# RMSNorm and matmul on one core: a reordered opening, a third load cut in two, and a last tile stored in two blocks

## The chip, the core and the metric

The kernel runs on one core of one Trainium2 chip. The metric is the device time of one execution in microseconds (us), median of several runs. The profile shows one execution; its span is some 1.8 us shorter than the time of the same run. A run's state is "fast" or "slow", or "unknown" where a kernel ran only once; the slow ones are left out of comparisons.

## The reference

```python
batch, seq, dim, out_dim = 16, 1024, 512, 768
rms = np.sqrt(np.mean(x ** 2, axis=-1, keepdims=True) + eps)
x_norm = x / rms * gamma
return np.matmul(x_norm, weight).astype(np.float32)
```

x has 16384 rows of 512 floats. The kernel works on 128 tiles of 128 rows. It reads 35 MB and writes 50 MB.

## The kernel before

Gamma is multiplied into the weights once, and each row's 1/rms is applied to the finished product. So a tile of x needs a cast to bf16, transposes on TensorE (PE), eight matmuls (four chunks of 128 rows of weights, each in a block of 512 and one of 256 columns), and one scaling on its way from PSUM to the output tile. PE can only start on the real work when the first weights have been loaded, cast and multiplied. This is the opening:

```python
    opening = [1, 2, 1, 2, 2]
    x_first, x_size = stretches(XG, {0: opening + [4, 4], 1: [4, 4, 8]})
    o_first, o_size = stretches(OG, {0: opening, 1: [4, 4], last - 1: [4, 4], last: [2, 2, 2, 1, 1]})
    ...
        load_until(3)                      # x tile 0, then tiles 1 and 2 in one load
        for h in range(2):                 # then the two halves of the weights
            nc.sync.dma_start(out=w_f32[:, 2 * h:2 * h + 2, :].rearrange("p c o -> p (c o)"), in_=wv[:, h, :])
        load_until(2 * XG)
    ...
        weights(0, nc.vector, 0, WIDE)     # chunk 0 on DVE, in two blocks
        weights(0, nc.vector, WIDE, O)
        weights(1, nc.scalar)              # chunk 1 on ACT
        for k in (0, 1):
            for i in range(3):
                matmuls(i, acc[i], [k])
        root(0, 3, ssq)
        weights(2, nc.vector)
        weights(3, nc.scalar)
        ...
        matmuls(0, acc[0], [2, 3])
```

x comes in groups of 16 tiles with two buffers, so the third group (tiles 32 to 47) can be loaded only when the first group has been used. All loads of x and weights and all stores go out from SyncE (SP). At the end, tiles 126 and 127 are computed in two column blocks (512 on ACT, 256 on DVE) and stored whole.

## Time and profile before

| what | before |
|---|---|
| time, 6 runs | 210.96 us (210.69 to 211.86) |
| span of the profiled run | 208.6 us |
| PE busy | 199.0 us (95%) |
| first real matmul | 8.67 us |
| end of the last compute | 203.58 us |

The page of the profile cuts the span into 40 slices; a digit is the busy share of one slice in tenths.

### The profile page before, as it was taken

How to read it: one execution, taken by the hardware profiler on the slowest of the kernel's cores; microseconds unless marked ns; L12 is line 12 of the kernel's file. 1: busy time of each engine (PE TensorE's matmuls, PEld its weight loads, DVE VectorE, ACT ScalarE, POOL GpSimd, SP SyncE). 2: the span in 40 equal slices, each digit the busy share in tenths (PEclk: the TensorE clock that was granted, in tenths of full speed). 3: DMA queues.
4: the chain of work that ended last, by engine and by line, in shares of the span. 5: the costliest groups of instructions: out<-in, count | busy, mean ns of one | idle time of the engine just before them, and what ended most of it. 6: DMA issues, size and time to landing. Idle time of an engine off the chain costs nothing.

```text
span 208.6 us, 3553 instructions
## 1 busy us (share of the span) xinstructions
PE 199.0 (95%) x1268; PEld 137.7 (66%) x1293; DVE 111.6 (54%) x204; ACT 158.2 (76%) x388; POOL 65.8 (32%) x71
## 2 busy tenths in 40 slices
PE   7799999999999999999999999999999999999990
PEld 3366777666766776677667666766776667667650
DVE  2555654654564465456546545654664565456450
ACT  4589787787778778777877877787787778778850
POOL 1058532303631343215323063311533054230000
PEclk9999999999999999999999999999999999999999
DMA  6999999999999999999999999999999999899885
GB/s 216 399 431 415 424 398 433 478 408 394 438 448 421 410 438 434 440 412 424 448 437 432 396 438 438 434 412 432 438 427 456 405 424 437 353 443 386 361 349 225
DMA packets 6630, 85.69 MB, mean 411 GB/s; under 512 B 978, under 2 KB 980, under 8 KB 3156
## 3 DMA queue, kind: packets, MB, share of 16 engines
q1 hardware_dynamic: 6336, 85.46, 97.0%
q8 instruction: 10, 0.16, 0.3%
q10 hardware_dynamic: 276, 0.00, 0.1%
q14 instruction: 8, 0.07, 0.1%
HBM read 35.13 MB, written 50.33 MB: 410 GB/s over the span
## 4 chain that ended last, share of the span: by engine, by line
PE 91%; DMA 3%; DVE 1%; ACT 1%; issue 1%; SPq 0%; DVEq 0%
PE ops L156 78%; PE tp L121 13%; DMA w_f<-in_weight_dram 3%; DVE ot L140 1%; ACT ot L138 0%; SPq L83 0%; ACT jk L98 0%; DVE w_bf L140 0%; DVE xT L128 0%; ACT rms L102 0%; DVE rstd L104 0%; DVEq L140 0%
## 5 line engine op out<-in xcount | busy, mean ns | idle before, releaser
L156 PE MATMUL ops<-w_bf,xT 128*128 128x512 bf16 (+1 forms) x999 | 192.5, 324 | 2.8 <-DVE w_bf L140 1.4
L156 PEld LDWEIGHTS <-xT 128*128 128x128 bf16 x1024 | 100.2, 98 | 57.8 <-issue 1.9
L94 POOL CAST xb<-xt 128x1024 bf16<-128x1024 f32 (+1 forms) x65 | 65.1, 1016 | 120.0 <-PE tp L121 62.2
L128 DVE COPY xT<-tp 128x1024 bf16<-128x1024 bf16 (+1 forms) x67 | 44.5, 667 | 81.0 <-PE tp L121 81.0
L138 ACT ACTIVATE ot<-ops,rstd 128x768 f32<-128x768 f32 (+1 forms) x65 | 58.1, 895 | 37.6 <-PE ops L156 36.8
L98 ACT ACTIVATE jk<-xt 128x512 bf16<-128x512 f32 x128 | 78.7, 619 | 1.1 <-DMA xt<-in_x_dram 1.1
L121 PE MATMUL tp<-ident_f,xb 128*128 128x128 f32 x256 | 69.2, 275 | 0.1
L140 DVE TENSOR_SCALAR ot<-ops,rstd 128x768 f32<-128x768 f32 (+1 forms) x65 | 64.5, 992 | 2.9 <-PE ops L156 2.8
L121 PEld LDWEIGHTS tp<-ident_f,xb 128*128 128x128 f32 x256 | 36.1, 142 | 3.8 <-issue 0.7
L98 ACT ACTIVATION_READ_ACCUMULATOR jk<-xt 128x1 f32 x128 | 24.4, 191 | 0.0
L102 ACT ACTIVATE rms<-ssq,eps_sb 128x2 f32<-128x2 f32 (+1 forms) x64 | 18.9, 296 | 2.0
L104 DVE RECIPROCAL rstd<-rms 128x2 f32<-128x2 f32 (+1 forms) x64 | 10.0, 156 | 3.3 <-ACT rms L102 3.2
L211 PE MATMUL ops<-warm 128*128 128x512 bf16 x11 | 4.8, 585 | 1.2 <-DVE eps_sb L204 1.2
L138 ACT ACTIVATE w_bf<-w_f,g_sb 128x768 bf16<-128x768 f32 x2 | 1.9, 936 | 2.6 <-DMA w_f<-in_weight_dram 2.6
L211 PEld LDWEIGHTS <-warm 128*128 128x128 bf16 x11 | 1.4, 134 | 2.6 <-issue 1.4
L193 ACT ACT_TABLE_LOAD x1 | 1.3, 1283 | 1.8 <-issue 1.8
L94 DVE CAST xb<-xt 128x512 bf16<-128x512 f32 x2 | 1.0, 491 | 2.4 <-DMA xt<-in_x_dram 2.4
L140 DVE TENSOR_SCALAR w_bf<-w_f,g_sb 128x512 bf16<-128x512 f32 (+2 forms) x3 | 1.4, 484 | 1.2 <-DMA w_f<-in_weight_dram 1.2
L225 PEld LDWEIGHTS tp<-ident_f,g_row 2*128 2x128 f32 x2 | 0.3, 201 | 0.8 <-issue 0.8
L202 DVE MEMSET warm<- 128x256 uint32 x1 | 0.3, 272 | 0.9 <-PEq L312 0.9
L225 PE MATMUL tp<-ident_f,g_row 2*128 2x2 f32 x2 | 0.4, 264 | 0.0
L227 DVE COPY g_sb<-tp 128x4 f32<-128x4 f32 x1 | 0.2, 161 | 0.4 <-PE tp L225 0.4
(7 smaller groups left out, 1.0 us busy)
## 6 DMA issues: line engine op xcount, KB each, us to landing
out_dram<-ot SPq DMA_DIRECT2D x12, 3072.0 KB, 15.1
xt<-in_x_dram SPq DMA_DIRECT2D x6, 4096.0 KB, 19.2
out_dram<-ot SPq DMA_DIRECT2D x4, 1536.0 KB, 10.8
out_dram<-ot SPq DMA_DIRECT2D x6, 768.0 KB, 9.6
xt<-in_x_dram SPq DMA_DIRECT2D x4, 1024.0 KB, 13.9
xt<-in_x_dram SPq DMA_DIRECT2D x1, 2048.0 KB, 18.8
xt<-in_x_dram SPq DMA_DIRECT2D x3, 512.0 KB, 6.2
w_f<-in_weight_dram SPq DMA_DIRECT2D x2, 768.0 KB, 7.1
```

Source lines behind the costliest of these rows:

```text
L94: engine.tensor_copy(out=xb_tiles[i // 2][:, i % 2:i % 2 + n, :], in_=held(x_tiles, XG, i, n))
L98: nc.scalar.activation(out=jk, in_=held(x_tiles, XG, i)[:, 0, :], func=AF.Square, accum_out=ssq)
L102: nc.scalar.activation(out=rms[:, :n], in_=ssq[:, :n], func=AF.Sqrt, scale=1.0 / D, bias=eps_sb)
L104: nc.vector.reciprocal(out=rstd[:, :n], in_=rms[:, :n])
L121: nc.tensor.transpose(out=tp_tiles[j][:, t, h, :], in_=words[:, lo:lo + P], identity=ident_f)
L128: nc.vector.tensor_copy(out=dst[:, t:t + n, :], in_=src[:, t:t + n, :])
L138: nc.scalar.mul(out=dst, in_=src, mul=r)
L140: nc.vector.tensor_single_scalar(out=dst, in_=src, scalar=r, op=mybir.AluOpType.mult)
L156: nc.tensor.matmul(out=acc[:, lo:hi], lhsT=xT_tiles[i // 2][:, i % 2, k // 2, :, k % 2], rhs=w_bf[:, k, lo:hi], start=(k == 0), stop=(k == ...
L193: nc.scalar.preload_act_table(AF.Sqrt)
L211: nc.tensor.matmul(out=spare[:, :WIDE], lhsT=warm[:, :P], rhs=warm, start=True, stop=True)
L225: nc.tensor.transpose(out=gp[:, c, :], in_=g_row[:, :, c], identity=ident_f[:2, :2])
```

## The change

The intent: the first half of the weights goes ahead of x tile 2, so that PE starts earlier and works on tiles 0 and 1 as they land; the third group of x comes in two loads; and the end is stored in smaller pieces, so that less is left to transfer after the last matmul. Before the weights, a tiny load "touches" them; it now goes ahead of gamma's load. The matmuls that only warm PE up are regrouped too (13 instead of 11; the cut below leaves them out).

```diff
-    opening = [1, 2, 1, 2, 2]
+    opening = [1, 1, 1, 1, 2, 2]
-    x_first, x_size = stretches(XG, {0: opening + [4, 4], 1: [4, 4, 8]})
-    o_first, o_size = stretches(OG, {0: opening, 1: [4, 4], last - 1: [4, 4], last: [2, 2, 2, 1, 1]})
+    x_first, x_size = stretches(XG, {0: opening + [4, 4], 1: [4, 4, 8], 2: [8, 8]})
+    o_first, o_size = stretches(OG, {0: opening, 1: [4, 4], last - 1: [4, 4], last: [2, 2, 1, 1, 1, 1]})
...  (touch of the weights moved ahead of the load of gamma)
+        load_until(2)
+        load_weights(0)
         load_until(3)
-        for h in range(2):
-            nc.sync.dma_start(out=w_f32[:, 2 * h:2 * h + 2, :]...)
+        load_weights(1)
         load_until(2 * XG)
...
         weights(1, nc.scalar)
-        for k in (0, 1):
-            for i in range(3):
-                matmuls(i, acc[i], [k])
+        cast(2, nc.gpsimd)
+        square(2, ssq[:, 2:3])
+        matmuls(0, acc[0], [0, 1])
+        transpose_tile(2)
+        matmuls(1, acc[1], [0, 1])
+        matmuls(2, acc[2], [0, 1])
+        weights(2, nc.vector)
         root(0, 3, ssq)
...
-            store(i)
+                if i == NT - 1:
+                    nc.sync.dma_start(out=rows(out, i, 1)[:, 0, lo:hi], in_=out_tile(i)[:, lo:hi])
+            if i < NT - 1:
+                store(i)
```

More of the change, by code (lines that the diff above doesn't have):

```diff
@@ L186 @@
     with tc.manual_schedule():
-        g_row = singles.tile([2, P, 2], F32)
-        nc.scalar.dma_start(out=g_row, in_=gamma.rearrange("(h w c) -> h w c", w=P, c=2))
         wv = weight.rearrange("(h w c) o -> w h (c o)", w=P, c=2)
@@ L192, with load_weights @@
         nc.scalar.dma_start(out=touched, in_=wv[:, :, 0:1])
+        g_row = singles.tile([2, P, 2], F32)
+        nc.scalar.dma_start(out=g_row, in_=gamma.rearrange("(h w c) -> h w c", w=P, c=2))
         nc.scalar.preload_act_table(AF.Sqrt)
+        w_f32 = singles.tile([P, K, O], F32)
+        def load_weights(h):
+            nc.sync.dma_start(out=w_f32[:, 2 * h:2 * h + 2, :].rearrange("p c o -> p (c o)"), in_=wv[:, h, :])
+        load_until(2)
+        load_weights(0)
         load_until(3)
-        w_f32 = singles.tile([P, K, O], F32)
-        for h in range(2):
-            nc.sync.dma_start(out=w_f32[:, 2 * h:2 * h + 2, :].rearrange("p c o -> p (c o)"), in_=wv[:, h, :])
+        load_weights(1)
         load_until(2 * XG)
@@ L227 @@
         nc.vector.tensor_copy(out=g_sb, in_=gp)
+        cast(1, nc.vector)
+        square(1, ssq[:, 1:2])
         transpose_tile(0)
-        warm_up(3)
-        cast(1, nc.vector)
-        cast(2, nc.gpsimd)
-        square(1, ssq[:, 1:2])
-        square(2, ssq[:, 2:3])
+        warm_up(2)
         transpose_tile(1)
-        transpose_tile(2)
-        warm_up(2)
+        warm_up(5)
         acc = [accumulator() for _ in range(4)]
@@ L241 @@
         weights(1, nc.scalar)
-        for k in (0, 1):
-            for i in range(3):
-                matmuls(i, acc[i], [k])
+        cast(2, nc.gpsimd)
[5 more added lines that the diff above has]
+        weights(2, nc.vector)
         root(0, 3, ssq)
-        weights(2, nc.vector)
         weights(3, nc.scalar)
@@ L250 @@
         finish_tile(0, acc[0], nc.scalar)
+        matmuls(1, acc[1], [2, 3])
         transpose_tile(3)
+        finish_tile(1, acc[1], nc.vector)
         norms(3, 1)
-        matmuls(1, acc[1], [2, 3])
-        finish_tile(1, acc[1], nc.vector)
         cast(4, nc.gpsimd)
```

## The prediction

> **What bounds the kernel now.** I read the page first, for the engine that is full and for the two ends of the row of slices.
>
> ```profile
> PE 199.0 (95%) x1268; PEld 137.7 (66%) x1293; DVE 111.6 (54%) x204; ACT 158.2 (76%) x388; POOL 65.8 (32%) x71
> ...
> PE   7799999999999999999999999999999999999990
> ...
> PE 91%; DMA 3%; DVE 1%; ACT 1%; issue 1%; SPq 0%; DVEq 0%
> ```
>
> TensorE (PE) is busy nine tenths or more of every slice but the first two and the last, and it carries 91% of the chain that ended last. The middle can be checked by windows: 49.63, 49.69 and 39.69 us of PE work in windows of 50, 50 and 40 us. A pair of tiles repeats every 3.03 us whatever the transfers do. So the middle has nothing to give, and I looked only at the time before PE's real work starts and after it stops. The timeline of the first microseconds gives the start:
>
> ```profile
> 6.65 0.59 PE L211 MATMUL ops<-warm 128*128 128x512 bf16 x2
> ...
> 8.12 0.94 ACT L138 ACTIVATE w_bf<-w_f,g_sb 128x768 bf16<-128x768 f32 x1 [1.90 <-DMA w_f<-in_weight_dram]
> 8.13 0.75 DVE L140 TENSOR_SCALAR w_bf<-w_f,g_sb 128x512 bf16<-128x512 f32 x2 [0.75 <-DMA w_f<-in_weight_dram]
> 8.67 1.51 PE L156 MATMUL ops<-w_bf,xT 128*128 128x512 bf16 x8 [1.43 <-DVE w_bf L140]
> ...
> 9.93 0.94 ACT L138 ACTIVATE w_bf<-w_f,g_sb 128x768 bf16<-128x768 f32 x1 [0.68 <-DMA w_f<-in_weight_dram]
> 9.93 0.62 DVE L140 TENSOR_SCALAR w_bf<-w_f,g_sb 128x768 bf16<-128x768 f32 x1 [0.48 <-DMA w_f<-in_weight_dram]
> ```
>
> The columns are start, duration, engine, line, operation, and in brackets the idle time before it with its releaser. PE is idle 1.43 us until the first half of the weights has landed (8.03 to 8.1) and its first block is cast (8.63). From 8.67 on PE does not stop. The second half lands at 9.9 and is cast by 10.55 (DVE, chunk 2) and 10.87 (ACT, chunk 3). PE's six tile halves on the first weights take 6 x 0.325 us (0.216 + 0.108 us for 512 and 256 columns) and end at about 10.62. So PE asks for chunk 2 just 0.07 us after it is ready: **the two arrivals are balanced**, and this decides my estimate.
>
> At the other end I read the timeline and windows of half a microsecond:
>
> ```profile
> 202.67 0.69 ACT L138 ACTIVATE ot<-ops,rstd 128x512 f32<-128x512 f32 x1 [0.61 <-PE ops L156]
> 203.10 0.48 DVE L140 TENSOR_SCALAR ot<-ops,rstd 128x256 f32<-128x256 f32 x1 [0.81 <-PE ops L156]
> ```
> ```profile
> 201.50:202.00 0.50, 0.50 (x5) 0.29 (x3) 0.22 (x2) 0.50 (x1) 0.00 (x0) 1.00 0.72 283
> 202.00:202.50 0.50, 0.50 (x4) 0.23 (x3) 0.29 (x1) 0.06 (x1) 0.00 (x0) 1.00 0.45 184
> 202.50:203.00 0.50, 0.50 (x5) 0.26 (x3) 0.00 (x0) 0.33 (x1) 0.00 (x0) 1.00 1.01 418
> ...
> 206.00:206.50 0.50, 0.00 (x0) 0.00 (x0) 0.00 (x0) 0.00 (x0) 0.00 (x0) 1.00 0.69 264
> 206.50:207.00 0.50, 0.00 (x0) 0.00 (x0) 0.00 (x0) 0.00 (x0) 0.00 (x0) 1.00 0.06 25
> ```
>
> The last two columns are DMA share and GB/s. Compute ends at 203.58, the span at 208.6: 5 us of storing. The transfers run at full rate from 202.5 to 206.3, so there is a backlog, preceded by a hole of some 0.35 us of full work (shares 0.72 and 0.45).
>
> **What the Trainium skill says.** "DMA: Bandwidth & Descriptors", section "Queues, rings and completion order": all copies issued by one sequencer share one ring on each of 16 DMA engines, and each engine consumes its ring in order[...]. It adds that the engines finish independently, so a copy is done when its slowest engine is. The trace agrees with both. In its completion records, 14 of 16 engines had finished the first half of the weights by 6.92 us, the other two at 7.87 and 8.03; for the second half, 14 by 8.79, two at 9.74 and 9.90. The packets show two engines standing still from about 4.8 to 5.9 after one packet of the weights, and carrying that lag of 1.1 us along. The same page, "Anatomy of one DMA", puts a fixed 2 us on a copy, mostly the receipt of the last write (fitted there to the GpSimd path). Here the first x tile, 256 KB, took 2.76 us from issue to use; at the 0.085 us that a 2 KB packet takes, 8 packets per engine are 0.68 us of it, so about 2 us is fixed. "TensorE: Matmul & The Clock Gate", Part 1, says that PE runs at half clock until it has been busy for some 3.4 us; here the warm-up matmuls took 634 ns early and 379 ns late.
>
> **The change part by part.**
>
> *Order of loads.* One tile of x (8 packets of 2 KB per engine, 8 x 0.085 = 0.68 us) goes ahead of the weights in place of two (8 packets of 4 KB, 8 x 0.159 = 1.27). The first half of the weights lands 0.59 us earlier: 8.03 becomes 7.44. Tile 2 then costs 0.68 between the halves, so the second half lands 0.09 later, at about 10.0: nothing was taken out ahead of it.
>
> *Start of PE.* The casts take as long as before (8.03 to 8.67 = 0.64), so the first matmul is at 8.08. Tile 0 runs chunks 0 and 1 at once, and chunk 1 comes from ACT 0.94 + 0.1 us after landing, at 8.48; tile 0 ends its half at 8.81. Tile 2 of x lands at 7.44 + 0.68 = 8.12, its cast on GpSimd takes 0.61, so its transposes fit right after at 8.83 (0.22 us), then tiles 1 and 2 (2 x 0.325 x 2 = 1.3): PE is through at 10.35.
>
> *The wait that replaces it.* Chunk 2 is cast at 10.0 + 0.05 + 0.62 = 10.67, chunk 3 at about 11.0. PE waits some 0.3 us, and finishes tile 0 at about 11.33. Before, it finished tile 0 at 10.62 + 0.65 = 11.27, having done the transposes of tile 2 in the idle time. From there on both kernels have the same PE work. So the opening **gains nothing as long as the second half arrives at 10.0**; the 0.59 us is taken back as 0.3 us of waiting, 0.22 us of transposes moved into the busy stretch and 0.1 us of waiting for chunk 1. Net: +0.05 us.
>
> *Touching the weights first, gamma second.* The touch goes out 0.57 us earlier, as do the weights themselves, so their distance is the same. Gamma used to arrive at 2.8 and PE asked for it at 3.86: about 1 us of slack. Even if it waits behind the 256 tiny pieces of the touch, which landed 3.7 us after issue, it comes near 5, and the second cast is at about 5.3, where it was before (5.25). Cost 0.
>
> *Third group in two loads.* The second half is asked for four pairs later, still six pairs (18 us) before its first cast. PE does not idle there before (23.84 us busy of the 24 after 26 us). Worth 0.
>
> *End.* Tile 124 is stored alone and fills the hole of 0.35 us. The last tile's wide block leaves at 203.4 rather than 203.63, but it queues behind the backlog. Rows of 3, 2 and 1 KB cost a little more per byte (0.121 us for 3 KB against 0.236 for 6 KB, and a further issue of 0.33 us): about 0.1 us back. For most engines this is 0.2 us gained. But the span waits for the last engine: on the final store 15 engines completed by 206.87 and one at 207.65, and that one had no hole (it completed its shares at 203.33, 205.48, 206.75 and 207.65). For it the gain is near 0. I take 0.1.
>
> Sum: +0.05 - 0.1 = -0.05 us, so 210.87 for this reading.
>
> **Rivals.**
>
> *The standstill goes away.* If the two engines stop because the first reads of the weights meet the touch (its 4-byte packets run at 4.0 to 4.6, right before), a changed order could remove it. Then the second half lands at 8.8, chunk 2 is cast at 9.45, PE is through its six halves at about 9.5 (limited by the five warm-ups, until about 7.4), and the gain is 1.1 to 1.3 us: 209.6. For it: the coincidence, and that two engines alone are hit. Against it: touch and weights move together by 0.57 to 0.59 us, and other lags of about 1 us appear later in the run with no touch. I give it 30%.
>
> *Late or cold start.* If gamma arrives after 5.5, or the gap while PE waits for it keeps the clock at half rate, the five warm-ups take 5 x 0.427 = 2.1 us and run into the first real work, or the first matmuls run at half speed: 0.2 to 0.5 us lost, 211.2. For it: fewer warm-ups ahead. Against: PE still has 5 at the end. 10%.
>
> *Lag at the end instead of the hole.* If no engine lags at the end, the last store gains 0.3 us more: 210.5. It adds to either case and widens the lower side.
>
> **Range and chances.** 0.6 x 210.85 + 0.3 x 209.6 + 0.1 x 211.2 = 210.5. The runs of before scatter over 0.3 us. The range covers the second case and the third: 209.4 to 211.2. A gain of 2% would be 4.2 us, almost all of PE's 8.67 us of start; a loss of 2% would need a new stall in the middle. Faster 0.01, same 0.98, slower 0.01.
>
> **What would show it right or wrong.** Right: the first real matmul of PE near 8.1 instead of 8.67; then an idle of about 0.3 us before 10.7, released by the cast of chunk 2; completion of the second half of the weights near 10.0; the same 3.03 us per pair; no hole in the transfers near 202, and compute's end to span's end still 4.8 to 5 us. Wrong: the second half of the weights completing near 8.8 (the standstill gone, gain over 1 us); PE waiting for gamma beyond 5.5; the first matmuls taking twice their time; or any idle of PE in the middle.

## The result

The changed kernel takes 210.82 us (210.66 to 211.39, 6 runs), the kernel before 210.96 us. The ratio is 0.9994, 95% interval 0.9972 to 1.0016: the same. Executions over 1.5% slower than the fastest of the same kernel are left out of the means. A ratio here is the mean time of one kernel's fast runs over that of the other's of the same rounds, so it is not quite the ratio of the medians quoted.

The page of the changed kernel, busy times and chain of waits:

```profile
PE 200.0 (96%) x1295; PEld 137.5 (66%) x1295; DVE 111.5 (53%) x204; ACT 158.3 (76%) x388; POOL 65.8 (31%) x71
...
PE 89%; DMA 3%; ACT 3%; DVE 1%; SPq 1%; issue 0%
```

Nothing has moved much at this scale. The start has. First the chain of the kernel before in its first microseconds (start, duration, what), then that of the changed kernel:

```profile
1.64 6.39 DMA w_f<-in_weight_dram
...
8.13 0.50 DVE w_bf L140
8.67 2.82 PE ops L156 x16
```
```profile
2.59 7.29 DMA w_f<-in_weight_dram
9.90 0.63 DVE w_bf L140
10.57 0.82 PE ops L156 x4
```

In the kernel before, the chain runs through the *first* half of the weights (issued at 1.64). In the changed kernel it runs through the *second* half (issued at 2.59), and PE joins the chain only at 10.57. The bound has passed from one arrival to the next. The timeline of the changed kernel shows the rest (start, duration, engine, line, operation, idle before):

```profile
8.00 0.92 PE L156 MATMUL ops<-w_bf,xT 128*128 128x512 bf16 x4 [1.47 <-DVE w_bf L140]
8.75 0.41 PE L121 MATMUL tp<-ident_f,xb 128*128 128x128 f32 x2
...
7.46 0.75 DVE L140 TENSOR_SCALAR w_bf<-w_f,g_sb 128x512 bf16<-128x512 f32 x2 [1.55 <-DMA w_f<-in_weight_dram]
9.90 0.62 DVE L140 TENSOR_SCALAR w_bf<-w_f,g_sb 128x768 bf16<-128x768 f32 x1 [0.27 <-DMA w_f<-in_weight_dram]
```

PE starts at 8.00 instead of 8.67. The single matmul records give what follows: the last matmul on the first half of the weights starts at 10.23 and lasts 0.11, and the first on the second half starts at 10.57, a wait of 0.23 us. Tile 0 is through PE at 11.22 us, against 11.32 before. So 0.67 us of earlier start leave 0.10 us, and this is still what is left at the end of the run. The last scalings of the changed kernel:

```profile
202.57 0.69 ACT L138 ACTIVATE ot<-ops,rstd 128x512 f32<-128x512 f32 x1 [0.61 <-PE ops L156]
203.01 0.48 DVE L140 TENSOR_SCALAR ot<-ops,rstd 128x256 f32<-128x256 f32 x1 [0.82 <-PE ops L156]
```

Both start 0.1 us earlier than before (202.67 and 203.10). But the span is 208.9 us, 0.3 longer. Windows of half a microsecond (the last two columns are DMA share and GB/s):

```profile
202.00:202.50 0.50, 0.50 (x5) 0.25 (x4) 0.19 (x1) 0.00 (x0) 0.00 (x0) 1.00 1.06 430
...
206.50:207.00 0.50, 0.00 (x0) 0.00 (x0) 0.00 (x0) 0.00 (x0) 0.00 (x0) 0.50 0.19 74
207.00:207.50 0.50, 0.00 (x0) 0.00 (x0) 0.00 (x0) 0.00 (x0) 0.00 (x0) 0.50 0.17 57
```

The hole at 202 us is gone (430 GB/s where 184 stood). In its place there is a tail: after 206.5 us the share is 0.19 and 0.17, which is three engines of 16. In the trace's completion records, 13 of 16 engines have finished the last store by 206.30, and the other three at 207.72, 207.80 and 207.87. In the kernel before it was 206.77 for thirteen, 206.87 for fifteen and 207.65 for the last. The hole was filled, for the engines that nobody waits for.

### The profile page after: what moved, and what is told of

Read it like the earlier page. It is cut to its first block, busy times and chain, and to the rows that moved or that the text cites. A ratio compares the mean times of both kernels' runs of the same rounds, so it can differ in the third digit from the quotient of the medians.

```text
span 208.9 us, 3591 instructions
## 1 busy us (share of the span) xinstructions
PE 200.0 (96%) x1295; PEld 137.5 (66%) x1295; DVE 111.5 (53%) x204; ACT 158.3 (76%) x388; POOL 65.8 (31%) x71
## 4 chain that ended last, share of the span: by engine, by line
PE 89%; DMA 3%; ACT 3%; DVE 1%; SPq 1%; issue 0%
PE ops L156 76%; PE tp L121 13%; DMA w_f<-in_weight_dram 3%; ACT jk L98 1%; ACT ot L138 1%; SPq L83 1%; ACT rms L102 0%; DVE xT L128 0%; DVE w_bf L140 0%; DVE ot L140 0%; SPq L197 0%; DVE rstd L104 0%
## 5 line engine op out<-in xcount | busy, mean ns | idle before, releaser
L156 PE MATMUL ops<-w_bf,xT 128*128 128x256 bf16 (+1 forms) x1024 | 194.4, 326 | 1.8 <-DVE w_bf L140 1.5
## 6 DMA issues: line engine op xcount, KB each, us to landing
xt<-in_x_dram SPq DMA_DIRECT2D x4, 1024.0 KB, 13.2
out_dram<-ot SPq DMA_DIRECT2D x4, 768.0 KB, 10.6
```

Of the source, the lines that this page charges most:

```text
L156: nc.tensor.matmul(out=acc[:, lo:hi], lhsT=xT_tiles[i // 2][:, i % 2, k // 2, :, k % 2], rhs=w_bf[:, k, lo:hi], start=(k == 0), stop=(k == ...
```

## The experiments

Twelve kernels ran.

### The opening alone

The changed kernel with the old end and the old third group:

```diff
-{..., 1: [4, 4, 8], 2: [8, 8]}    ...last: [2, 2, 1, 1, 1, 1]}
+{..., 1: [4, 4, 8]}               ...last: [2, 2, 2, 1, 1]}
```

> The changed opening (loads in the order x0, x1, first half of the weights, x2, second half; touch before gamma; the new order of work) with the old end and the old third group. Theory 1 (second half decides): first real matmul at 8.0 to 8.1 us instead of 8.67, second half of the weights still used at 9.9 to 10.0, last matmul of PE within 0.15 us of before; time within 0.1% of before. Rival (the opening is worth its 0.6 us and the changed end loses it): PE stops about 0.6 us earlier than before and the time is 0.3% lower, about 210.3.

Measured: 211.0 us (210.32 to 211.39) against 210.68, ratio 1.0004 (0.9974 to 1.0034). The rival's gain of 0.3% (a ratio of 0.997) lies just below the interval, too close to its edge to rest on. The profile settles it:

```profile
8.80 0.92 PE L156 MATMUL ops<-w_bf,xT 128*128 128x512 bf16 x4 [2.30 <-DVE w_bf L140]
...
10.74 0.62 DVE L140 TENSOR_SCALAR w_bf<-w_f,g_sb 128x768 bf16<-128x768 f32 x1 [0.30 <-DMA w_f<-in_weight_dram]
...
204.49 0.48 DVE L140 TENSOR_SCALAR ot<-ops,rstd 128x256 f32<-128x256 f32 x1 [0.82 <-PE ops L156]
```

PE started at 8.80, the second half of the weights was first used at 10.74, and the last scaling began at 204.49 instead of 203.10. PE did not even start earlier than in the kernel before. The arrival of the weights was not where theory 1 put it; it was 0.8 us later. But PE followed it, as theory 1 says. (In this profile no DMA engine lagged at the end: all 16 completed the last store between 208.04 and 208.27.) PE also lost 0.59 us at x tile 32, of which more below.

### The end alone

```diff
-last: [2, 2, 2, 1, 1]
+last: [2, 2, 1, 1, 1, 1]      (and the last tile stored in two column blocks)
```

> Only the changed end (tiles 124 and 125 stored alone, last tile in two column blocks) on the kernel before. Theory 1 (the slowest DMA engine decides): no hole in the transfers around 202 us, 13 engines complete the last store some 0.4 to 0.6 us earlier than before (206.3 instead of 206.87), but the last engine completes at 207.4 to 208.0, and the time is within 0.1% of before. Rival (the hole counts): the last engine too completes 0.3 us or more earlier than 207.65 and the time is 0.15% or more lower.

Measured: 210.96 us (210.3 to 211.44) against 210.68, ratio 0.9998 (0.997 to 1.0026). Thirteen engines completed the last store by 206.44, the last one at 207.80. Both are as theory 1 had it: the hole was filled, the slowest engine gained nothing.

This profile also brought what nobody had looked for. By luck, its weights came early (second half used at 9.01, first matmul at 7.67, a whole microsecond ahead of before): no DMA engine lagged, and all 16 had landed the first half between 6.64 and 7.00 us. Yet the last scaling began at 203.13. Its timeline, PE and GpSimd (POOL):

```profile
52.13 0.33 PE L121 MATMUL tp<-ident_f,xb 128*128 128x128 f32 x1 [0.79 <-POOL xb L94]
...
51.03 2.03 POOL L94 CAST xb<-xt 128x1024 bf16<-128x1024 f32 x2 [11.31 <-DMA xt<-in_x_dram]
```

PE stood still before the transposes of x tile 32, waiting for a cast that waited for the third group of x. In the kernel before and in the changed kernel the same cast reads:

```profile
50.38 3.01 POOL L94 CAST xb<-xt 128x1024 bf16<-128x1024 f32 x3 [9.68 <-DMA xt<-in_x_dram]
```
```profile
47.05 3.01 POOL L94 CAST xb<-xt 128x1024 bf16<-128x1024 f32 x3 [6.45 <-DMA xt<-in_x_dram]
```

Before, the first cast takes until 51.42 and PE needs it at 52.16, so there was 0.74 us of slack and no wait. With the group in two loads there are 4 us of slack. The 0.74 us is no fixed floor, though: it holds for one profile. With the group in one load, the eighth of the 16 DMA engines completed it at 48.01 us before, 47.86 here and 48.01 with the opening alone; the last one at 50.23, 50.88 and 52.24. The cast waits for the last, so the stall too hangs on the engine that lags.

### Without the second half of the weights

Wrong on purpose, once on each kernel:

```diff
-        load_weights(1)                                  # before: range(2) becomes range(1)
-            scale(engine, w_bf[:, k, lo:hi], w_f32[:, k, lo:hi], ...)
+            scale(engine, w_bf[:, k, lo:hi], w_f32[:, k % 2, lo:hi], ...)
```

> Wrong result on purpose: the kernel before without the load of the second half of the weights; chunks 2 and 3 are cast from the first half. It takes the second arrival away. Theory 1 (before was balanced: PE asked for chunk 2 0.07 us after it was there): first matmul still at 8.67, last matmul of PE at most 0.1 us earlier than the 203.1 of before. Rival (the second half held before up too): 0.3 us or more earlier.

> Wrong result on purpose: the changed kernel without the load of the second half of the weights; chunks 2 and 3 are cast from the first half. Theory 1 (the second arrival takes the gain): PE does not wait between 10.2 and 10.6 us any more, and its last matmul ends 0.2 to 0.35 us earlier than in the changed kernel (there about 203.0). The rest of the 0.67 us stays lost in the transposes of tile 2 (0.22 us) and the wait for chunk 1. Rival (something else, such as the cast of x tile 2, holds PE): less than 0.1 us earlier.

These were single runs (210.93 and 210.37 us), and their openings differ in luck, so I compare each with its own first matmul. On the changed kernel: from the first matmul (8.89) to the last scaling (203.70) 194.81 us, against 195.01 (8.00 to 203.01) with the second half. The gain is 0.20 us, the lower end of theory 1's range and twice the rival's most. Two other profiles with the new opening have 195.04 and 195.10 us for this stretch (the stall at tile 32 taken off), so 0.20 us is more than their spread. PE's records show no wait between the halves. On the kernel before, 195.10 us (8.63 to 203.73) against 194.43: 0.67 us *longer*. Its first matmuls ran at half speed until about 10.2 us (631 ns for one of 512 columns where 379 is normal), and the first three pairs of matmuls took 1.69 us where the kernel before took 1.02. That is the whole 0.67 us, so nothing is left for the second half, as the balance has it. But this is one run with a correction larger than the effect looked for: weak support, no proof.

### A faster opening, with the third group whole and cut

The weights are loaded and cast in four chunks, and matmuls follow chunk by chunk:

```diff
-        load_weights(0)                 +        load_chunk(0); load_chunk(1)
         load_until(3)                            load_until(3)
-        load_weights(1)                 +        load_chunk(2); load_chunk(3)
+        chunk(0); matmuls(0, acc[0], [0]); matmuls(1, acc[1], [0])
+        chunk(1); matmuls(0, acc[0], [1]); matmuls(1, acc[1], [1])
+        ...transpose_tile(2); matmuls(2, acc[2], [0, 1]); chunk(2) ...
```

> The changed kernel with an opening made faster still (weights loaded and cast in four chunks, each chunk used for the tiles at hand as it lands) but with the third group of x in one load as before. Theory 1b, formed on the one profile in which the old opening happened to be 1 us early and PE then lost that 1 us at 51 us (waiting for the cast of x tile 32): with the third group in one load PE cannot pass tile 32 before about 51.5 us. First matmul near 7.5, a stall of 0.5 to 1.5 us of PE just before the transposes of tile 32 (51 to 52.5 us), PE's last matmul not earlier than 203.0, time within 0.2% of before. Rival (the stall was chance): no stall, PE ends near 202.3.

> The same faster opening with the third group of x in two loads, as in the change. Theory 1b: no stall at 51 us, PE's last matmul 0.5 to 0.9 us earlier than in the changed kernel (203.0), so near 202.3; how much of it the end of the span keeps depends on the backlog of stores, between 0 and 0.9 us, so 209.9 to 210.8. Rival (third group worth 0): same as the version with the single load.

Measured: 211.27 us with the third group whole (ratio 1.0015, 0.9981 to 1.0049) and 211.37 with it cut (1.0028, 0.999 to 1.0066). The opening was not faster, and the forecast of 209.9 to 210.8 us for the second version failed: its last scaling began at 203.59, not near 202.3. In it PE started at 6.35 but then waited for chunk 1 (1.1 us) and, having no more work on tiles 0 and 1, for the transposed tile 2 (first matmul on it at 9.84). In the change, tile 1's matmuls fill just that gap. So this was no version to beat either kernel. The stall came out as theory 1b has it: with the group whole PE lost 0.84 us before tile 32 (6.91 us instead of 6.07 for the eight transposes up to it), with the group cut nothing.

### The third group cut, alone

> The kernel before with only the third group of x in two loads. Theory 1b: PE reaches tile 32 at about 52.1 us in the kernel before, when its cast is ready at 51.4, so the split removes no wait there unless the opening happens to be early: tile 32's cast some 3 us earlier (47 to 48 us), PE's end unchanged for the same start, time within 0.15% of before. Rival (the single load costs time anyway, for instance by holding the stores behind it): 0.2% or more faster.

Measured: 210.88 us (210.34 to 211.61) against 210.95, ratio 0.9997 (0.9965 to 1.0029). No stall; the last scaling at 202.95 after a second half used at 9.79. On its own the part is worth nothing that can be measured, as predicted.

### Finer stores towards the end

```diff
-last - 1: [4, 4], ...
+last - 3: [4, 4], last - 2: [2, 2, 2, 2], last - 1: [2, 2, 2, 2], ...
```

> The changed kernel with only the stores of tiles 96 to 119 cut finer (8, 8, 4 and 4 tiles become 4, 4, then twos). Theory 2: the bursts of large stores leave the DMA engines without work around 180, 193 and 199 us and with a backlog at the end, which the engine that lags pays for; with finer stores the holes near 181 and 193 are filled, every engine has caught up by 200, and after the last compute (203.5) the last engine completes near 206 instead of 207.9. Span 206.8 to 207.6, time 1.0 to 2.0 us lower than the changed kernel. Rival (a fixed cost of ending, no backlog): less than 0.4 us.

The fast runs lie at 210.85 to 211.19; ratio 1.0002 (0.9973 to 1.003). The 1 to 2 us of theory 2 did not come, so its forecast failed. Whether the finer stores filled the holes, and where the expected gain went, is not shown.

### Relieving every DMA engine

One look suggested a reason for the flat times so far. The packet records of both kernels show moments after 180 us when most engines have nothing to do: around 181, 193, 200 and, in the kernel before, 202 us. At least three of the 16 engines were still at work in each of these holes. The records do not name the engine, so that it is the same ones each time is inferred. The completions fit: in the kernel before, the last of 16 trails the thirteenth by 0.5 to 2.2 us in every transfer on record from 28 us to the end. Such an engine never runs dry, and it completes last. To test this I removed one store of 3 MB in the middle of the run, on both kernels. Nothing that PE waits for is touched (wrong: tiles 64 to 71 are not written):

```diff
-        if i == first + n - 1:
+        if i == first + n - 1 and first != 64:
```

> Wrong result on purpose: the changed kernel without the store of tiles 64 to 71 (3 MB, 8 packets of 0.912 us per DMA engine, so 7.3 us of each engine's time at about 110 us). Nothing that PE waits for is touched. Theory 3, formed on the profiles so far, in which at every hole of the transfers after 180 us two to four DMA engines were still at work and one of them completed last: the slowest DMA engine sets the end, not PE. With 7.3 us taken from every engine the lag is gone before the end: from the end of the last compute to the end of the span 4.0 to 4.4 us instead of 5.4, the last engine within 0.3 us of the thirteenth, time 0.8 to 1.3 us lower (ratio 0.994 to 0.996). Rival (the end is a fixed cost after PE's last matmul): 5.2 to 5.6 us as before, time within 0.2 us.

> Wrong result on purpose: the kernel before without the store of tiles 64 to 71. Theory 3: the same relief: from the last compute to the end 4.1 to 4.5 us instead of 5.0. And with the slowest DMA engine out of the way the change is bare: the changed kernel without this store should then be 0 to 0.4 us faster than this one, the hole of 0.35 us at 202 us being there only here. Rival: no relief, and the two stay equal.

| profile | last compute ends | 13 engines done | last engine | span | compute's end to span's end |
|---|---|---|---|---|---|
| before | 203.58 | 206.77 | 207.65 | 208.6 | 5.0 |
| changed | 203.49 | 206.30 | 207.87 | 208.9 | 5.4 |
| before, without the store | 203.75 | 206.92 | 206.95 | 208.0 | 4.3 |
| changed, without the store | 204.17 | 206.94 | 207.57 | 208.6 | 4.4 |

Without the store, the kernel before takes 209.62 us (209.48 to 209.81) against 210.73: ratio 0.9933 (0.990 to 0.9966). In the profile PE ends no earlier than before, yet the medians are 1.1 us apart and the profiled spans 0.6. Around 181 us every engine now runs dry, where before some were at work (the kernel before, then the one without the store):

```profile
181.00:181.50 0.50, 0.50 (x5) 0.40 (x4) 0.00 (x0) 0.30 (x1) 0.00 (x0) 1.00 0.35 147
```
```profile
181.00:181.50 0.50, 0.50 (x6) 0.35 (x4) 0.10 (x2) 0.14 (x1) 0.00 (x0) 1.00 0.00 0
```

The store issued next, at 181 us, is completed by the thirteenth engine at 189.87 us and by the last at 191.95 before, and at 189.74 and 189.90 without the store: the lag of 2.1 us is gone. In the last windows the tail is missing:

```profile
206.00:206.50 0.50, 0.00 (x0) 0.00 (x0) 0.00 (x0) 0.00 (x0) 0.00 (x0) 1.00 0.90 350
206.50:207.00 0.50, 0.00 (x0) 0.00 (x0) 0.00 (x0) 0.00 (x0) 0.00 (x0) 1.00 0.01 0
```

So in the kernel before, the backlog of the slowest DMA engine, and not PE's last matmul alone, sets the end. Theory 3 is shown there. On the changed kernel the way from compute to the end shrinks by 1.0 us as expected (5.4 to 4.4), but 0.7 us of this is compute ending later. The last engine completes 0.3 us earlier than with the store, and still 0.6 us after the thirteenth, where I expected 0.3. The time gains less: 210.39 us (209.59 to 211.34), ratio 0.997 (0.9935 to 1.0006). The interval includes both no gain and the gain I expected, so theory 3 is not shown for the changed kernel by its time.

And with the store left out of both, the changed kernel is not 0 to 0.4 us faster than the kernel before but 0.77 us slower in the medians. Its runs also scatter over 1.75 us, those of before over 0.33. That expectation failed, and it points at the opening: in the two profiles the changed kernel used the second half of the weights 1.47 us later (10.58 against 9.11), and its compute ended 0.42 us later although the kernel before lost 0.90 us at tile 32.

### Is it the touch, or the order of loads?

The last run put gamma back ahead of the touch:

```diff
+        nc.scalar.dma_start(out=g_row, ...)      # gamma first again
         nc.scalar.dma_start(out=touched, in_=wv[:, :, 0:1])
-        nc.scalar.dma_start(out=g_row, ...)
```

> Wrong result on purpose: the changed kernel without the store of tiles 64 to 71 and with gamma loaded before the touch of the weights, as in the kernel before. Without that store the slowest DMA engine does not hold the end, so the time shows the opening: 210.39 us with touch first and the new load order, 209.62 with gamma first and the old load order. In the profiles so far the second half of the weights was first used at 9.0 to 9.9 us with the old opening (four profiles) and at 9.9 to 11.0 with the new one (four). Theory 4a (the touch going first delays the weights): near 209.6, second half used at 9.0 to 9.9. Theory 4b (the new load order does it, the weights following after one x tile instead of two): near 210.4, second half used at 10.3 or later.

The four fast runs are 208.79, 210.28, 210.89 and 211.54 us (two more were slow, and so was the profile). Putting gamma first again does not bring back the steady 209.6 of the old opening. This speaks against 4a and for 4b, but with a scatter of 2.75 us it does not settle the matter.

### Sending one store over fewer engines

```diff
+            for lo, hi in ((0, 120), (120, 128)) if first == 64 else ((0, 128),):
+                nc.sync.dma_start(out=rows(out, first, n)[lo:hi], in_=held(o_tiles, OG, first, n)[lo:hi])
```

> The changed kernel with one store (tiles 64 to 71) sent as 120 partitions and 8 partitions. By the Trainium skill (DMA: Bandwidth & Descriptors, Why a DMA increments its semaphore by 16 and not by 1) the first goes over the 15 lowest engines, the second over 8, so the highest engine is spared 7.3 us of work and eight engines get 0.9 us more. Theory 3 with the highest engine among the slow ones: the last completions come 0.5 us or more earlier, or one engine fewer lags at the end; time 0 to 1 us lower. If the slow ones are other engines: no change, or up to 0.9 us slower. It is a try at a version that beats both.

Measured: 217.43 us, ratio 1.0302 (1.0255 to 1.0349). The completion records agree with the count of engines in the expectation: 15 for the large piece, 8 for the small one; which engines these were they do not tell. After that store, pieces of 24 KB took 1.29 to 1.49 us on average instead of 0.91 between 128 and 140 us, the transfers fell to 318 GB/s from 130 to 140 us, and PE then waited 5 us for x and had half the clock granted for 6.8 us (from 152.7 us). The try failed, and why one uneven store slows the transfers for some 20 us is not known. It does show again how little spare room the transfers have.

## Why the prediction was right or wrong

The time was predicted at 210.5 with 210.87 for the main reading, and came out at 210.82; the chance of "same" was right. That the main reading came within 0.05 us is partly luck: the runs of either kernel scatter over 0.7 us or more, and openings differ by a microsecond from profile to profile. By its steps:

- **Order of loads.** Right in the profile of the changed kernel: the first half in use at 7.44 to 7.46, as predicted, and the second at 9.90 against 10.0. But that was luck. In the four other profiles of the new order with its weights in halves and not known to be slow, the first half was in use only at 8.09 to 8.55 us, if anything later than with the old order (7.09 to 8.12). What the reordering did reliably is hidden behind the slowest engine: the eighth of the 16 DMA engines completed the first half at 5.73 to 6.08 us instead of 6.66 to 6.82, which is 0.75 us earlier on average (predicted: 0.59). The last one lagged more: 1.6 to 2.4 us behind the eighth instead of 0.2 to 1.3.
- **The wait that replaces it.** Right in kind and nearly in size: 0.23 us of waiting for chunk 2 (predicted 0.3), 0.25 us for the transposes of tile 2 in the busy stretch (0.22). The net was a gain of 0.10 us instead of a loss of 0.05, since before PE had reached chunk 2 at 10.67 rather than 10.62 and the casts after the change came a little sooner. The runs show the rule behind it well. In seven profiles with whole halves of the weights, the start of the last scaling minus the first use of the second half, minus the stall at tile 32 where there was one, is nearly the same:

| profile | second half used | last scaling | stall at tile 32 | remainder |
|---|---|---|---|---|
| before | 9.93 | 203.10 | 0 | 193.17 |
| changed | 9.90 | 203.01 | 0 | 193.11 |
| opening alone | 10.74 | 204.49 | 0.59 | 193.16 |
| end alone | 9.01 | 203.13 | 0.96 | 193.16 |
| third group alone | 9.79 | 202.95 | 0 | 193.16 |
| changed, store left out | 10.58 | 203.69 | 0 | 193.11 |
| before, store left out | 9.11 | 203.27 | 0.90 | 193.26 |

  Within one order this proves little, as the two halves land at nearly the same distance each time. The comparison of the orders does: counted from the first matmul, the remainder is 194.43 to 194.50 us with the old order and 195.01 to 195.10 with the new one, 0.6 us apart; counted from the second half, they agree. When PE finishes is settled by when the second half of the weights comes and by the stall at tile 32.

- **Third group, "Worth 0".** Right for this time, wrong as a reading. I looked for a wait, found none, and did not measure the slack, which was 0.74 us. In four of the five later profiles with the single load it was used up. Twice this took back a lucky opening (the end alone 0.96 us, before without the store 0.90). The opening alone lost 0.59 us although it had started late, since its last engine landed the group 2 us later than in the kernel before; the four-chunk opening lost 0.84.
- **The end.** Right, with the step that mattered named: the hole is filled, the last engine had no hole. The term of 0.1 us gained was too friendly; the last engine completed 0.2 us later than before. What I did not see is how far this reaches: the lag is not an accident of the last stores, since some engines were at work in every hole. Relieving them is worth 1.1 us to the kernel before.
- **Touch and gamma.** The cost of 0 was right. Gamma came at 3.2 us, so the worst case of 5 did not arise. That touch and weights keep their distance was wrong: most of the touch's packets moved from 4.2 to 4.6 us to 2.4 to 3.0, the weights' first packet only from 4.35 to 3.29.
- **Rival "the standstill goes away".** It did not go away with the touch. The touch's tiny packets now end before the weights' first one, and still one 6 KB packet of the weights took 1025 ns at 4.08, others 540 to 850. And in the profile of the end alone, where the touch runs right before the weights as in the kernel before, no packet of theirs took over 450 ns, and the second half landed at 8.98: the rival's arrival, by luck and in the old order. So the touch alone does not explain the lag. I had also described the standstill loosely: before, the two engines did not stand still, they sat in one packet each of 1416 and 1518 ns (normal: 234).
- **Rival "late or cold start".** It did not happen in this profile, but the two slow profiles of later runs had it: the granted clock fell to half for 3.4 us at the first matmuls.
- **Two slips.** A gain of 4.2 us would be about half of PE's 8.67 us of start, not almost all of it. And what the prediction quotes on engines finishing independently stands in another section of that page, "Why a DMA increments its semaphore by 16 and not by 1". Nothing rests on either.

What stays open: why the slowest DMA engines lagged more with the new load order. With whole halves and a fast state, the four profiles with the old order had the second half in use at 9.0 to 9.9 us; the four with the new order (the changed kernel, the opening alone, the changed kernel without the store, and the one with the uneven store) at 9.9, 10.7, 10.6 and 11.0. By the queue it should be 0.09 us later. With so few profiles, chance is not excluded. No version was found that is correct and beats both kernels.

## What to carry to other kernels

When two arrivals stand one behind the other, taking time off the first moves the wait to the second; before counting a gain, ask when the next thing must be there, and write down its slack, not only whether it waits today. When the row of an engine and the DMA row are both full, look at when the slowest of the 16 DMA engines completes each transfer: here it set the start of PE's work, the stall at tile 32 and, in the kernel before, the end, and filling holes for the other engines gained nothing. A test that removes work which no compute waits for showed this clearly on the kernel before. And one profile of an opening is one draw: take several before calling an arrival early.

## What the Trainium skill lacked or had wrong

- No page has that single packets take far longer than their neighbours: 1416 and 1518 ns for 6 KB packets of the weights where 234 is normal. Since a copy has landed only when all its engines have finished ("DMA: Bandwidth & Descriptors", Why a DMA increments its semaphore by 16 and not by 1, with which the trace agrees: 14 of 16 by 6.92 us, the last at 8.03), two such packets cost the whole first half 1.1 us. Nor has any page how long such a lag lives: in the kernel before, from 28 us to the end.
- No page says how often the core's own instruction fetches come and what they cost the DMA engines. Here 10 packets of 16 KB come about every 19 us (at 156.9, 175.6 and 193.4 us in the kernel before); that last one took 1012 ns, and a store packet of 12 KB starting as it ended took 1432 instead of 460 (that both were on one engine is inferred from the times).
- "Why a DMA increments its semaphore by 16 and not by 1" of "DMA: Bandwidth & Descriptors" explains how many engines a copy uses (15 and 8 here, and the records agree), but not what an uneven split may do to those behind it: here 318 GB/s instead of 430, and 6.6 us more in all.
- "TensorE: Matmul & The Clock Gate", Part 1, puts the return to the half clock after an idle window of about 3.4 us. In one slow run (gamma first, store left out) the clock stood at 0.50 from 9.8 to 13.2 us after PE had idled for only 1.86 us; in the opening alone, PE idled for 2.30 us and the clock stayed full.
